# The gain of the first norm: one row spread by a product with ones, and products of the identity ahead of the first tokens

## The chip, the core and the metric

The kernel runs on one NeuronCore of a Trainium2 chip. The metric is the device time of one execution in microseconds. Three runs of the kernel before the change gave 1168.95, 1169.08 and 1169.35 us; the median, 1169.08, is the time before.

## The reference, cut to what matters

One inference step of a hybrid layer, in f32, over 1024 prompt tokens and 8 sample tokens, with 1024 channels:

```
y = xf * lax.rsqrt(jnp.mean(xf * xf, axis=-1, keepdims=True) + EPS) * g      # rms_norm
...
h = rms_norm(x, norm_g)
proj = jnp.einsum('btd,de->bte', h, w_in)
rq, rk, rv, rg, sq, sk, sv, sg, mg_r, mg_s = jnp.split(proj, _split_points(), axis=-1)
rq = rope(rq...); rk = rope(rk...) * (RET_DK ** -0.5)
o_r, ret_state = retention_fn(rq, rk, rv)                                    # branch A, 4 heads
...
y = x + jnp.einsum('btd,de->bte', merged, w_out)
```

The change touches only `norm_g`, the 1024 weights `g` of the first norm: how they come to stand in each of the 128 partitions.

## The kernel before, in words

**Tiles and stages.** The prompt is cut into tiles of 128 tokens, 0 to 7; tile 8 is the 8 sample tokens. `norm_h` (L255) is called once for each. It loads the tile `x` by a DMA on SP's queue (L266), squares it on ScalarE with a sum along the row (L275; two instructions in the trace, the pass and the reading of the sum), makes the root: VectorE the mean (`ms`, L145), GpSimd the power (`rs`, L146). Then VectorE multiplies the tile by the root and by the gain `self.gb` in one pass (L281); for tile 6 alone (`XPOOL`) GpSimd multiplies by the gain (L278) and ScalarE by the root (L279). TensorE transposes the tile in two halves of four products with the identity (L286) into PSUM tiles `tr`, of which there are two. ScalarE copies each half into `hhi`, rounded to the TensorE type fp32r (L138), and VectorE writes what the rounding left out into `hlo` (L139). So each product of activations and weights is made of three: high by high, low by high, high by low.

**The gain.** In tile 0's call, right behind the load of `x`, a DMA reads `norm_g` with a broadcast to 128 partitions into the tile `st` (L267 to L269). All nine tiles use it.

**Weights.** `load_unit` (L150) loads a unit into `wraw` (three buffers), ScalarE writes `whi` (L167), GpSimd `wlo` (L168). The k and v weights of head 0 are four units of 384 KB (128 columns of k, 256 of v, two DMAs each), the q weights one unit of 512 KB.

**Work of TensorE at the start.** For each tile of tokens 24 products of 128x384 (`gemm_tok`, L221 to L223) make k and v; for each block of 344 tokens 24 products of 128x344 (`gemm_T`, L211 to L213) make q, which `ret_q` (L318) turns on VectorE in three passes (L325 to L327) and adds on GpSimd (L328). Both write into PSUM tiles `acc`, of which there are three. Block 0 of q needs the tokens of tiles 0 to 2, block 1 those of tiles 2 to 5. The raw k and v weights of head 0 come a second time as `rraw` (1.5 MB, `load_rows`, L241) for the sample rows, whose products (`quad_rows`, L249) need tile 8. `begin` (L754) sets up the tables; the list `steps` (L787) says in which order the program emits norms, unit loads and tables.

**Order and buffers.** What each engine does in which order is not the order of emission: the framework's scheduler places every instruction when the program is built (`schedule_with_timeline_sim=True`), and the orders are fixed then. Tiles 0 and 1, 2 and 3, 5 and 6, 7 and 8 share a pair buffer `oT` (two of them, `xpair`); tile 4 uses a `qT` buffer. All loads of the start stand in SP's queue, one behind the other.

**Later phases.** Eight groups (four retention heads, four groups of windowed attention) with gates and merge gates, then the branch projections and the output projection.

Of the kernel before, what the change touches and what calls it, by code (L numbers as in the profile page):

```python
# [18 lines left out]
P = 128  # L19
D = 1024  # L20
# [30 lines left out]
NMISC = 8 + 8 + 2 + 2  # L51

RAW = 3
NA1 = 7
XQ = 4
XPOOL = (6,)
# [65 lines left out]
class Body:  # L122
# [27 lines left out]
    def load_unit(self, spec):  # L150
        nc = self.nc
        kind, segs, k0, nk = spec
        width = sum(w for _, _, w in segs)
        raw = self.t(self.wp, [P, D], "wraw", bufs=RAW)
        hi = self.t(self.wp, [P, D], "whi", F32R, bufs=self.wbufs)
# [99 lines left out]
    def norm_h(self, t):  # L255
        nc = self.nc
        p = P if t < NT else NS
        cs = slice(t * P, t * P + p)
# [5 lines left out]
                self.xpair = self.t(self.gp, [P, 2, TOK], "oT", bufs=2)  # L264
            x = self.xpair[:, i % 2, :D]
        nc.sync.dma_start(out=x[:p], in_=self.i["x_prompt"][0, cs, :] if t < NT else self.i["x_sample"][:, 0, :])  # L266
        if t == 0:  # L267
            self.gb = self.t(self.ap, [P, D], "st", bufs=1)
            nc.sync.dma_start(out=self.gb[:], in_=self.i["norm_g"][0:1, :].broadcast_to([P, D]))  # L269
        if t < NT:  # L270
            junk = self.hhi[:, :, cs]
        else:
# [9 lines left out]
        for half in range(2):  # L282
            ps = self.t(self.ptr, [P, 4, P], "tr")
# [433 lines left out]
    def groups(self):  # L717
        nc = self.nc
# [9 lines left out]
        def use(name):  # L728
            if self.apctx is not None:
                self.apctx.__exit__(None, None, None)  # L730
            self.apctx = self.tc.tile_pool(name=name, bufs=1, side="right", reuse_waits="tile") if name else None
            if name:
                self.ap = self.apctx.__enter__()
# [17 lines left out]
        kv = slabs([(OFF_RK, DK), (OFF_RV, DV)])  # L751
        qu = tch(OFF_RQ)

        def begin(us):  # L754
            use("ret")
            self.ropeT = self.t(self.ap, [P, 2, TOK], "ropeT")
            self.ropeK = self.t(self.ap, [P, NT + 1, 128], "ropeK")
            self.maskT = self.t(self.ap, [P, RH, P], "maskT")
            self.kst = self.t(self.ap, [KST, DK], "kst", F32R)
            self.vst = self.t(self.ap, [KST, DV], "vst", F32R)  # L760
            nc.gpsimd.memset(self.kst[:].bitcast(F32), 0.0)
            nc.gpsimd.memset(self.vst[:].bitcast(F32), 0.0)
            self.zq = self.t(self.ap, [P, 2, NS // 2, QD], "zq", bufs=1)
            nc.gpsimd.memset(self.zq[:], 0.0)
# [31 lines left out]
        for gi in range(8):  # L796
            ret = gi < 4
            st = {"v": None}
# [65 lines left out]
        def open_a(us):  # L864
# [3 lines left out]
            self.opA = []  # L868
            for k in range(0, NA1, 2):
                st = self.t(self.gp, [P, 2, TOK], "oT", bufs=2)  # L870
# [162 lines left out]
```

## Time and profile before

| what | value |
|---|---|
| median of the runs | 1169.08 us (1168.95 to 1169.35) |
| profiled execution: its own time, its span | 1167.54 us, 1165.8 us |
| mean granted TensorE clock of it | 0.996 |
| PE busy | 1142.7 us, 98%, 7140 instructions |
| PEld (weight loads) | 1088.8 us, 93% |
| DVE, ACT, POOL | 644.0 us (55%), 437.4 us (38%), 427.5 us (37%) |
| instructions in all | 19287 |
| HBM | 127.8 MB, 110 GB/s over the span |

PE is TensorE, PEld its weight loads, DVE VectorE, ACT ScalarE, POOL GpSimd, SP the engine whose queue issues the loads. A share is that of the whole span; the start of the program, which the change touches, is a few per cent of it and has to be read by itself. The clock is the one that the throttle granted to TensorE, as a share of full speed, 2.4 GHz; the low level is 1.2 GHz.

### The profile page before, as it was taken

The page shows a single profiled execution, that of the slowest core. Times are in us where ns is not written, and L with a number is a line of the kernel's source. Part 1 is how long each engine was busy: PE and PEld are TensorE (multiplying, and loading weights), DVE is VectorE, ACT ScalarE, POOL GpSimd, SP SyncE. Part 2 cuts the span into 40 slices and gives each one's busy share as a digit, 9 for nine tenths or more (in the row PEclk, how much of TensorE's full clock was granted, in tenths as well). Part 3 has the DMA queues.
Part 4 walks back from the last instruction along what each step waited for, and adds up shares of the span by engine and source line. Part 5 has one row for each costly group of instructions (what it writes and reads, how often), then busy time and mean ns, then how long its engine had stood idle before and what let it go on. Part 6 is the DMA issues. An engine that isn't in the chain of part 4 may idle for free.

```text
span 1165.8 us, 19287 instructions
## 1 busy us (share of the span) xinstructions
PE 1142.7 (98%) x7140; PEld 1088.8 (93%) x7140; DVE 644.0 (55%) x1823; ACT 437.4 (38%) x1130; POOL 427.5 (37%) x398
## 2 busy tenths in 40 slices
PE   6899999999999999999999999999999999999998
PEld 5899999999999999999999999999999999999876
DVE  5664645655644487767765776577744411665131
ACT  5444343334344244544463445345544210221010
POOL 4425116316225434634463446235751221221010
PEclk9899999999999999999999999999999999999999
DMA  9434315413123412311141114102437754546431
GB/s 319 124 111 130 115 43 165 154 60 100 47 81 104 141 32 59 91 60 31 34 133 44 33 33 139 38 1 64 151 115 249 230 152 130 179 139 206 158 101 64
DMA packets 135565, 126.99 MB, mean 109 GB/s; under 512 B 17768, under 2 KB 121576, under 8 KB 135440
## 3 DMA queue, kind: packets, MB, share of 16 engines
q1 hardware_dynamic: 128560, 117.32, 32.2%
q10 hardware_dynamic: 6912, 8.46, 2.0%
q8 instruction: 56, 0.92, 0.3%
q14 instruction: 37, 0.30, 0.1%
HBM read 95.37 MB, written 32.44 MB: 110 GB/s over the span
## 4 chain that ended last, share of the span: by engine, by line
PE 90%; DVE 4%; DMA 2%; issue 1%; ACT 1%; POOL 1%; SPq 0%; ACTq 0%; POOLq 0%
PE acc L211 16%; PE acc L212 16%; PE acc L213 15%; PE acc L221 10%; PE acc L223 10%; PE acc L222 10%; PE sc L550 1%; PE sc L551 1%; DMA oT<-in_x_prompt 1%; PE av L583 1%; PE av L582 1%; PE tr L562 1%; DMA oT<-d_o 1%; PE acc L249 1%; PE sc L201 1%
## 5 line engine op out<-in xcount | busy, mean ns | idle before, releaser
L168 POOL TENSOR_TENSOR wlo<-wraw,whi 128x1024 fp32r<-128x1024 f32 (+1 forms) x92 | 205.9, 2245 | 292.3 <-ACT whi L167 291.6
L211 PE MATMUL acc<-hhi,whi 128*128 128x344 f32 x864 | 279.5, 323 | 3.6 <-DVE rng L885 2.5
L212 PE MATMUL acc<-hlo,whi 128*128 128x344 f32 x864 | 277.8, 322 | 0.0
L213 PE MATMUL acc<-hhi,wlo 128*128 128x344 f32 x864 | 276.9, 321 | 0.0
L221 PE MATMUL acc<-whi,hhi 128*128 128x384 f32 x512 | 176.8, 346 | 2.3 <-DVE tg L302 1.2
L222 PE MATMUL acc<-wlo,hhi 128*128 128x384 f32 x512 | 176.1, 344 | 0.0
L223 PE MATMUL acc<-whi,hlo 128*128 128x384 f32 x512 | 175.8, 343 | 0.0
L211 PEld LDWEIGHTS acc<-hhi,whi 128*128 128x128 f32 x864 | 162.4, 188 | 6.1 <-ACT whi L167 2.7
L212 PEld LDWEIGHTS acc<-hlo,whi 128*128 128x128 f32 x864 | 162.4, 188 | 1.7 <-issue 0.4
L213 PEld LDWEIGHTS acc<-hhi,wlo 128*128 128x128 f32 x864 | 162.4, 188 | 1.0
L167 ACT ACTIVATE whi<-wraw 128x1024 fp32r<-128x1024 f32 (+1 forms) x92 | 90.3, 984 | 166.6 <-PE acc L212 110.4
L146 POOL TENSOR_TENSOR rs<-ms,nhalf 128x1 f32<-128x1 f32 (+3 forms) x81 | 68.6, 848 | 229.0 <-DVE ms L145 226.5
L221 PEld LDWEIGHTS acc<-whi,hhi 128*128 128x128 f32 x512 | 97.8, 191 | 5.1 <-issue 1.4
L223 PEld LDWEIGHTS acc<-whi,hlo 128*128 128x128 f32 x512 | 97.9, 191 | 0.9 <-issue 0.4
L222 PEld LDWEIGHTS acc<-wlo,hhi 128*128 128x128 f32 x512 | 98.0, 191 | 0.6 <-issue 0.2
L304 POOL TENSOR_TENSOR oT<-oT,tg 128x344 f32<-128x344 f32 x48 | 48.3, 1007 | 63.1 <-DVE tg L302 52.4
L504 ACT ACTIVATE s<-sc,ng,rs 128x128 f32<-128x128 f32 x128 | 56.9, 455 | 23.1 <-DVE ng L501 22.8
L223 PE MATMUL acc<-whi,mlo 128*128 128x512 f32 x128 | 50.5, 395 | 0.0
L221 PE MATMUL acc<-whi,mhi 128*128 128x512 f32 x128 | 50.4, 394 | 0.0
L222 PE MATMUL acc<-wlo,mhi 128*128 128x512 f32 x128 | 50.3, 393 | 0.0
L1000 DVE TENSOR_TENSOR x<-acc,x 128x512 f32<-128x512 f32 x16 | 11.1, 692 | 71.0 <-PE acc L223 71.0
L302 DVE SCALAR_TENSOR_TENSOR tg<-tg,acc 128x344 f32<-128x344 f32 x48 | 24.5, 510 | 31.8 <-ACT tg L301 31.6
(363 smaller groups left out, 2343.0 us busy)
## 6 DMA issues: line engine op xcount, KB each, us to landing
wraw<-in_w_in SPq DMA_DIRECT2D x36, 512.0 KB
d_t<-tg ACTq DMA_DIRECT2D x48, 172.0 KB
d_o<-oT SPq DMA_DIRECT2D x16, 516.0 KB
tt<-d_t SPq DMA_DIRECT2D x48, 172.0 KB
wraw<-in_w_in SPq DMA_DIRECT2D x32, 256.0 KB
st<-d_o SPq DMA_DIRECT2D x9, 516.0 KB
d_m<-tt SPq DMA_DIRECT2D x24, 172.0 KB
mm<-d_m SPq DMA_DIRECT2D x24, 172.0 KB
```

The costliest lines, as they stand in the source:

```text
L146: nc.gpsimd.tensor_tensor(out=rs[:p, :width], in0=ms[:p, :width], in1=self.nhalf[:p, :width], op=ALU.pow)
L167: nc.scalar.activation(out=hi[:, :f], in_=raw[:, :f], func=AF.Copy)
L168: nc.gpsimd.tensor_tensor(out=lo[:, :f], in0=raw[:, :f], in1=hi[:, :f].bitcast(F32), op=ALU.subtract)
L211: nc.tensor.matmul(ps, whi[:, k, :], hi[:, cs], start=(k == 0), stop=False)
L212: nc.tensor.matmul(ps, whi[:, k, :], lo[:, cs], start=False, stop=False)
L213: nc.tensor.matmul(ps, wlo[:, k, :], hi[:, cs], start=False, stop=(k == KT - 1))
L221: nc.tensor.matmul(ps, hi[:, k, a:b], whi[:, kk, :], start=(k == 0), stop=False)
L222: nc.tensor.matmul(ps, hi[:, k, a:b], wlo[:, kk, :], start=False, stop=False)
L223: nc.tensor.matmul(ps, lo[:, k, a:b], whi[:, kk, :], start=False, stop=(k == KT - 1))
L302: nc.vector.scalar_tensor_tensor(out=tg[:], in0=tg[:], scalar=1.0, in1=ps[:, :BL], op0=ALU.add, op1=ALU.mult)
L304: nc.gpsimd.tensor_tensor(out=sl, in0=sl, in1=tg[:], op=ALU.mult)
L504: nc.scalar.activation(out=s[:p, j, :], in_=src[j], func=AF.Exp, bias=ng[:p, j : j + 1], scale=scale[j], accum_out=l[:p, j : j + 1])
```

## The change

`norm_h` no longer allocates and loads the gain. A new function `spread_gain`, called first in `begin`, does it: one DMA brings `norm_g` as a row of 4 KB into one partition of the tile `zk`, GpSimd writes 128 ones behind it, and two products of the ones (one partition, 128 columns, as weights) with a half of the row (one partition, 512 columns) put the row into every partition of a PSUM tile `sc`, from which VectorE copies it into the two halves of `self.gb`. Beside them `WARM` = 9 products of the identity with itself go into a PSUM tile `av`, whose contents nothing reads. Since `begin` stands ahead of tile 0 in the list of steps, the row's DMA stands ahead of tile 0's.

```diff
--- before.py
+++ after.py
@@ -51,6 +51,7 @@
 NMISC = 8 + 8 + 2 + 2
 
 RAW = 3
+WARM = 9
 NA1 = 7
 XQ = 4
 XPOOL = (6,)
@@ -264,9 +265,6 @@
                 self.xpair = self.t(self.gp, [P, 2, TOK], "oT", bufs=2)
             x = self.xpair[:, i % 2, :D]
         nc.sync.dma_start(out=x[:p], in_=self.i["x_prompt"][0, cs, :] if t < NT else self.i["x_sample"][:, 0, :])
-        if t == 0:
-            self.gb = self.t(self.ap, [P, D], "st", bufs=1)
-            nc.sync.dma_start(out=self.gb[:], in_=self.i["norm_g"][0:1, :].broadcast_to([P, D]))
         if t < NT:
             junk = self.hhi[:, :, cs]
         else:
@@ -751,8 +749,24 @@
         kv = slabs([(OFF_RK, DK), (OFF_RV, DV)])
         qu = tch(OFF_RQ)
 
+        def spread_gain():
+            self.gb = self.t(self.ap, [P, D], "st", bufs=1)
+            row = self.t(self.ap, [1, D + P], "zk", bufs=1)
+            nc.sync.dma_start(out=row[:, :D], in_=self.i["norm_g"][0:1, :])
+            nc.gpsimd.memset(row[:, D:], 1.0)
+            ps = self.t(self.pav, [P, 512], "av")
+            warm = lambda n: [nc.tensor.matmul(ps[:, :P], self.ident[:], self.ident[:], start=True, stop=True) for _ in range(n)]
+            warm(WARM // 3)
+            for half in range(2):
+                cs = slice(half * 512, half * 512 + 512)
+                pg = self.t(self.psc, [P, 512], "sc")
+                nc.tensor.matmul(pg[:], row[:, D:], row[:, cs], start=True, stop=True)
+                nc.vector.tensor_copy(out=self.gb[:, cs], in_=pg[:])
+            warm(WARM - WARM // 3)
+
         def begin(us):
             use("ret")
+            spread_gain()
             self.ropeT = self.t(self.ap, [P, 2, TOK], "ropeT")
             self.ropeK = self.t(self.ap, [P, NT + 1, 128], "ropeK")
             self.maskT = self.t(self.ap, [P, RH, P], "maskT")
```

Line numbers: those of the changed kernel are one higher up to L253, two lower from `norm_h` on, and fourteen higher behind `begin`. The numbers that the framework gives to tiles move as well; each place below says which tiles they are.

The scheduler lays out the whole start anew. Three places show what stands where.

**VectorE, first rows behind the two memsets.** Of the kernel before (`oT_150` holds tiles 0 and 1, `st_152` is the gain, `ms_156`, `ms_185` are the means of tiles 0 and 1):

```order
L145 TENSOR_SCALAR ms_156<-ss_154 128x1
L281 SCALAR_TENSOR_TENSOR oT_150<-oT_150,rs_157,st_152 128x1024
L145 TENSOR_SCALAR ms_185<-ss_183 128x1
L139 TENSOR_TENSOR hlo_122<-tr_161,hhi_121 128x4x128
L281 SCALAR_TENSOR_TENSOR oT_150<-oT_150,rs_186,st_152 128x1024
L139 TENSOR_TENSOR hlo_122<-tr_168,hhi_121 128x4x128
```

Of the changed kernel (`st_141` is the gain, `sc_149` and `sc_152` its halves in PSUM, `ms_174`, `ms_203` and `ms_233` the means of tiles 0 to 2):

```order
L146 TENSOR_SCALAR ms_174<-ss_172 128x1
L146 TENSOR_SCALAR ms_203<-ss_201 128x1
L764 COPY st_141<-sc_149 128x512
L764 COPY st_141<-sc_152 128x512
L279 SCALAR_TENSOR_TENSOR oT_170<-oT_170,rs_175,st_141 128x1024
L279 SCALAR_TENSOR_TENSOR oT_170<-oT_170,rs_204,st_141 128x1024
L146 TENSOR_SCALAR ms_233<-ss_231 128x1
```

The copies of the gain stand behind the mean of tile 1, and the norm of tile 0 behind the copies; before, it stood behind its own mean.

**SP's queue, behind the loads of tiles 0 to 4 and of the first three k and v units.** Of the kernel before (`wraw_241` is the fourth k and v unit, `wraw_273` the q unit, `oT_302` tiles 5 and 6, `oT_349` tiles 7 and 8, `wraw_403` a later gate unit):

```order
L769 DMA ropeT_141<-in_c_ropeT 128x2x344 x2
L161 DMA wraw_241<-in_w_in 128x2x128
L161 DMA wraw_241<-in_w_in 128x2x256
L769 DMA ropeT_141<-in_c_ropeT 128x2x344
L241 DMA rraw_412<-in_w_in 128x8x128
L241 DMA rraw_412<-in_w_in 128x8x256
L161 DMA wraw_273<-in_w_in 128x8x128
L884 DMA rng_111<-in_ret_norm_g 128x8x1
L266 DMA oT_302<-in_x_prompt 128x1024 x2
L161 DMA wraw_403<-in_w_in 128x8x128
L266 DMA oT_349<-in_x_prompt 128x1024
L266 DMA oT_349<-in_x_sample 8x1024
```

Of the changed kernel (`wraw_259` is the fourth k and v unit, `wraw_291` the q unit, `oT_320` tiles 5 and 6, `oT_367` tile 7, `wraw_421` and `wraw_871` later gate units, `wraw_1199` the first unit of the next head):

```order
L162 DMA wraw_259<-in_w_in 128x2x256
L783 DMA ropeT_161<-in_c_ropeT 128x2x344 x3
L162 DMA wraw_291<-in_w_in 128x8x128
L242 DMA rraw_430<-in_w_in 128x8x128
L242 DMA rraw_430<-in_w_in 128x8x256
L898 DMA rng_111<-in_ret_norm_g 128x8x1
L162 DMA wraw_421<-in_w_in 128x8x128
L267 DMA oT_320<-in_x_prompt 128x1024 x2
L162 DMA wraw_871<-in_w_in 128x8x128
L162 DMA wraw_1199<-in_w_in 128x2x128
L162 DMA wraw_1199<-in_w_in 128x2x256
L267 DMA oT_367<-in_x_prompt 128x1024
```

The q unit has moved ahead of `rraw`; the gate unit has moved ahead of tiles 5 and 6; and one gate unit of 512 KB and a unit of 384 KB now stand ahead of tile 7, where one gate unit stood.

**VectorE and TensorE at tiles 5 to 8.** VectorE of the kernel before (`oT_302` with `rs_307` is tile 5, `tr_311` and `tr_318` its transposes, `oT_349` with `rs_354` tile 7 and with `rs_377` tile 8, `acc_495` block 0 of q):

```order
L281 SCALAR_TENSOR_TENSOR oT_302<-oT_302,rs_307,st_152 128x1024
L145 TENSOR_SCALAR ms_329<-ss_327 128x1
L145 TENSOR_SCALAR ms_353<-ss_351 128x1
L145 TENSOR_SCALAR ms_376<-ss_374 8x1
L139 TENSOR_TENSOR hlo_122<-tr_311,hhi_121 128x4x128
L281 SCALAR_TENSOR_TENSOR oT_349<-oT_349,rs_354,st_152 128x1024
L139 TENSOR_TENSOR hlo_122<-tr_318,hhi_121 128x4x128
L281 SCALAR_TENSOR_TENSOR oT_349<-oT_349,rs_377,st_152 8x1024
L325 TENSOR_TENSOR qT_410<-acc_495,ropeT_141 128x344
L326 TENSOR_TENSOR ropeu_520<-acc_495,ropeT_141 64x344
L327 TENSOR_TENSOR ropeu_520<-acc_495,ropeT_141 64x344
```

VectorE of the changed kernel (`oT_320` with `rs_325` is tile 5, `tr_329` and `tr_336` its transposes, `tr_306` and `tr_313` those of tile 4, `oT_367` with `rs_372` tile 7 and with `rs_395` tile 8, `acc_513` block 0 of q):

```order
L324 TENSOR_TENSOR ropeu_538<-acc_513,ropeT_161 64x344
L325 TENSOR_TENSOR ropeu_538<-acc_513,ropeT_161 64x344
L279 SCALAR_TENSOR_TENSOR oT_320<-oT_320,rs_325,st_141 128x1024
L146 TENSOR_SCALAR ms_347<-ss_345 128x1
L140 TENSOR_TENSOR hlo_122<-tr_306,hhi_121 128x4x128
L146 TENSOR_SCALAR ms_371<-ss_369 128x1
L279 SCALAR_TENSOR_TENSOR oT_367<-oT_367,rs_372,st_141 128x1024
L146 TENSOR_SCALAR ms_394<-ss_392 8x1
L140 TENSOR_TENSOR hlo_122<-tr_313,hhi_121 128x4x128
L279 SCALAR_TENSOR_TENSOR oT_367<-oT_367,rs_395,st_141 8x1024
L140 TENSOR_TENSOR hlo_122<-tr_329,hhi_121 128x4x128
L140 TENSOR_TENSOR hlo_122<-tr_336,hhi_121 128x4x128
```

TensorE of the changed kernel (`acc_604` is block 1 of q, `tr_353` the first half of tile 6):

```order
L284 MATMUL tr_329<-ident_63,oT_320 128x128 x4
L284 MATMUL tr_336<-ident_63,oT_320 128x128 x4
L212 MATMUL acc_604<-hhi_121,whi_292 128x344
L284 MATMUL tr_353<-ident_63,oT_320 128x128 x4
L213 MATMUL acc_604<-hlo_122,whi_292 128x344
L214 MATMUL acc_604<-hhi_121,wlo_293 128x344
L212 MATMUL acc_604<-hhi_121,whi_292 128x344
```

Block 0's rope now stands ahead of tile 5's norm, both norms of the second pair ahead of tile 5's low halves, and a half of tile 6's transposes between block 1's first and second product.

## Rows read from the trace of the kernel before

**Rows 1.** Stretch, length, busy PE, PEld, DVE, ACT, POOL, clock, DMA share, GB/s.
```profile
8.00:17.00 9.00, 7.91 (x29) 7.20 (x30) 4.64 (x7) 7.29 (x12) 7.43 (x5) 1.00 1.05 391
26.00:30.00 4.00, 1.52 (x11) 1.25 (x10) 3.93 (x17) 2.77 (x7) 0.03 (x1) 1.00 1.14 305
30.00:35.00 5.00, 5.00 (x20) 5.00 (x21) 2.26 (x2) 3.75 (x6) 5.00 (x3) 0.66 1.11 328
50.00:60.00 10.00, 10.00 (x59) 8.51 (x59) 5.33 (x21) 3.43 (x10) 0.00 (x0) 0.83 0.18 48
60.00:80.00 20.00, 20.00 (x135) 19.32 (x134) 12.44 (x47) 8.55 (x27) 6.10 (x8) 1.00 0.35 109
```

**Rows 2.** Timeline (start, duration, engine, operation, [idle before, releaser]): the first `rraw` product.
```profile
50.03 0.83 PE L249 MATMUL acc<-rraw,hx 128*8 128x384 f32 x8
```

**Rows 3.** Timeline: products of 128x384 in and behind slow stretches.
```profile
16.21 0.52 PE L222 MATMUL acc<-wlo,hhi 128*128 128x384 f32 x1
...
34.35 0.34 PE L223 MATMUL acc<-whi,hlo 128*128 128x384 f32 x1
```

**Rows 4.** Timeline, 28 to 36 us: block 0 of q, tiles 5 to 7.
```profile
28.84 1.05 ACT L167 ACTIVATE whi<-wraw 128x1024 fp32r<-128x1024 f32 x1
...
29.94 0.42 PE L211 MATMUL acc<-hhi,whi 128*128 128x344 f32 x1 [2.48 <-DVE rng L885]
...
29.97 2.39 POOL L168 TENSOR_TENSOR wlo<-wraw,whi 128x1024 fp32r<-128x1024 f32 x1 [5.02 <-ACT whi L167]
...
32.33 0.54 POOL L146 TENSOR_TENSOR rs<-ms,nhalf 128x1 f32<-128x1 f32 x1
...
32.84 2.39 POOL L278 TENSOR_TENSOR oT<-oT,st 128x1024 f32<-128x1024 f32 x1
32.90 3.42 DVE L281 SCALAR_TENSOR_TENSOR oT<-oT,rs,st 128x1024 f32<-128x1024 f32 x1 [1.60 <-POOL rs L146]
...
33.09 1.06 ACT L167 ACTIVATE whi<-wraw 128x1024 fp32r<-128x1024 f32 x1 [0.62 <-DMA wraw<-in_w_in]
...
34.56 1.06 ACT L275 ACTIVATE hhi<-oT 128x1024 fp32r<-128x1024 f32 x1 [0.41 <-DMA oT<-in_x_prompt]
```

**Rows 5.** Timeline, 0 to 10 us: the first loads and norms.
```profile
0.80 0.40 SPq L266 DMA_DIRECT2D oT<-in_x_prompt  x1
...
1.26 0.42 SPq L269 DMA_DIRECT2D st<-in_norm_g  x1
...
1.69 0.29 POOL masks.py:199 TENSOR_SCALAR_AFFINE_SELECT ident<-ident 128x128 f32<-128x128 f32 x1
...
4.56 1.06 ACT L275 ACTIVATE hhi<-oT 128x1024 fp32r<-128x1024 f32 x1 [2.48 <-DMA oT<-in_x_prompt]
...
6.80 1.28 DVE L281 SCALAR_TENSOR_TENSOR oT<-oT,rs,st 128x1024 f32<-128x1024 f32 x1 [0.90 <-DMA st<-in_norm_g]
...
9.37 1.06 ACT L275 ACTIVATE hhi<-oT 128x1024 fp32r<-128x1024 f32 x1 [0.41 <-DMA oT<-in_x_prompt]
```

**Rows 6.** Chain of waits (start, duration, what): two f32 products of 128x128.
```profile
60.73 0.22 PE av L391 x2
```

**Rows 7.** Timeline, 38 to 46 us: tiles 5 and 7, block 1 of q.
```profile
38.78 0.69 DVE L139 TENSOR_TENSOR hlo<-tr,hhi 128x512 fp32r<-128x512 f32 x1 [1.85 <-ACT hhi L138]
...
39.98 1.28 DVE L281 SCALAR_TENSOR_TENSOR oT<-oT,rs,st 128x1024 f32<-128x1024 f32 x1 [0.51 <-POOL rs L146]
...
40.59 0.60 PE L286 MATMUL tr<-ident,oT 128*128 128x128 f32 x4
...
40.94 0.40 PE L212 MATMUL acc<-hlo,whi 128*128 128x344 f32 x1
...
44.60 0.92 POOL L328 TENSOR_TENSOR qT<-qT,ropeu 128x344 f32<-128x344 f32 x1 [4.15 <-DVE ropeu L327]
...
44.94 0.31 PE L213 MATMUL acc<-hhi,wlo 128*128 128x344 f32 x1
...
45.76 0.51 DVE L325 TENSOR_TENSOR qT<-acc,ropeT 128x344 f32<-128x344 f32 x1
```

## The prediction

> **What bounds the kernel now.** I read the stretches first (busy time by window), then the start instruction by instruction. In the stretches [rows 1] the reader is to see that TensorE is busy 20.00 of 20.00 us from 60 us on, so nothing later can give time back, and that it is not full before: 7.91 of 9.00 us at 8 to 17, 1.52 of 4.00 at 26 to 30. The order of every engine is the same in both programs from about 100 us on, so the change is worth what it shifts the moment from which TensorE stays full. I take that moment at the first product on `rraw`, at 50.03 us [rows 2], with the same work done before it in both programs (tiles 0, 1, 2 of k and v, blocks 0 and 1 of q, all transposes).
>
> Three stretches run at 1.2 GHz. Single matmuls show it: 128x384 takes 0.52 us at 16.21 and 0.34 at 34.35 [rows 3]; the clock column of the first stretch reads 1.00 all the same, so there the rows of single matmuls decide. At 30 to 35 us the mean granted clock is 0.66, which is 3.4 us at half speed, and 0.83 at 50 to 60 is 3.4 us again [rows 1], which costs 1.7 us where TensorE is the bound. Before the spell at 31 us TensorE had stood idle for 2.48 us [rows 4].
>
> **The gain of the norm.** Before, its 512 KB stand second in SP's queue: issued at 1.26, and VectorE starts tile 0's norm at 6.80, the end of a wait for it [rows 5]. Tile 0 itself had landed at 4.56, so the broadcast held the queue for 2.24 us. Removed, everything behind it comes up to 2.24 us earlier, less 0.46 us because the row of 4 KB is now issued ahead of tile 0 (the step from 0.80 to 1.26 [rows 5]): 1.8 us.
>
> In its place stand nine products of the identity, two of ones with the row, and two copies. No row shows a product of 128x512 f32 on one partition. The nearest is the f32 product of 128x128, two instructions in 0.22 us at the high clock [rows 6]: 0.44 at the low one. Nine are 4.0 us; they begin when the identity is written (1.69 + 0.29 [rows 5]) and end at 6.0. The spread ones have four times the columns, 1.76 us each at the low clock and 0.88 at the high; by partitions used it could be less, not more. I take 1.76, since 8 to 17 us ran low after TensorE had begun: 7.8 and 9.5. The copies pass 512 columns out of PSUM as the 0.69 us pass does [rows 7]. On VectorE they stand behind tile 1's mean: tile 1 landed at 9.37 [rows 5], now 7.6, and its square takes 1.2, so the first copy starts at 8.9 and the second ends at 10.2. Then tile 0's norm, 1.28, would be done at 11.5 against 8.08. GpSimd's split of a weight unit lies beside it; a VectorE pass with two inputs in SBUF beside GpSimd's product of 2.39 us took 3.42 us [rows 4], so 12.8 is the upper end. Tile 0 comes **3.4 to 4.7 us later**, though its weights are there earlier.
>
> What hides that: q's weight unit (512 KB) now goes ahead of the 1.5 MB of `rraw`. Before, block 0 of q waited for it (weights at 28.84, TensorE idle 2.48 us to 29.94 [rows 4]) and block 0 with tile 2 ended at about 40.4, since the transposes behind block 1's first product start at 40.59 [rows 7]. Without that wait it is 37.9, and with the full 4.7 us on top 42.6. That is still no cost, if what follows it starts later than 42.6; it does.
>
> **Tile 5 and block 1 of q.** Block 1 needs tile 5. Before, tile 5's low half is made (0.69 us at 38.78) ahead of the norms of tiles 7 (39.98) and 8, and the block's second matmul runs at 40.94 [rows 7]. Now it stands behind both norms on VectorE, and TensorE has tile 6's transposes between the first and second matmul of the block, which need the buffer that this low half frees. The chain, from rows:
>
> Tile 5's norm ends at 36.3 (32.90 + 3.42 [rows 4]) as before: the unit that now stands just ahead of it in SP's queue has the place that q's had, with the same bytes ahead, so its split on GpSimd (29.97 + 2.39) and the product of tile 6 (to 35.2) stay where they are. Bounds: 34.5 if all of the 1.8 us reaches it, 37.2 if block 0's rope on VectorE, which now precedes it, is late. I take 36.3, by the bytes. GpSimd then has block 0's rope sum, 0.92 [rows 7], and two powers of 0.54 [rows 4]: 38.3. Tile 7 has 384 KB more ahead of it than before; 512 KB took 1.5 us there (33.09 to 34.56 [rows 4]), so it lands 1.1 us later, at 35.7, and its square is done at 36.9, inside 38.3. Tile 7's norm: 39.6. Tile 4's last low half 0.69, and a short mean: 40.5. Tile 8's norm 1.28: 41.8. Tile 5's low half 0.69: 42.5. Four transposes, 0.60 [rows 7]: the second matmul at **43.1 against 40.94, 2.2 us later**.
>
> From there to 50.03 the same matmuls and transposes follow. Two things differ. Before, block 1 ended at 45.25 and its rope began at 45.76, VectorE being busy; now it is free: 0.5 us back. And TensorE stands idle from the end of tile 2 (37.9 to 42.6) to 43.1, in the middle of that range about as long as the 2.48 us that preceded the spell at 31 us. I take the longer half, and so a low spell in block 1: 1.7 us. The spell after 50 us stays, since the idle time ahead of it is that of tiles 7 and 8 in both.
>
> **Sum**: 2.2 - 0.5 + 1.7 = 3.4 us later. The profiled execution took 1167.54 us, so 1170.9; the median of the runs shown stands 1.5 us above it, so **1172.5**. A measurement of this kernel can tell some 0.2%, 2.3 us, from no change. With the ends for tile 5 (1.8 earlier, 0.9 later) the sum goes from 1.6 to 4.3.
>
> **The rivals.**
> *The clock holds.* Block 1 finds the high clock, or the spell after 50 us does not return: 3.4 - 1.7 = 1.7 us, 1170.8, no difference that can be told. For it: TensorE's wait before block 1 may be as short as 0.5 us. Against: at 26 to 30 us a wait of 2.48 us was enough [rows 1, 4].
> *The front carries through* (faster). Transfers 2.24 us earlier move tile 5's norm as much, and block 0 ends early enough that its rope sum on GpSimd, 0.92, no longer stands ahead of tile 7's power. Then the second matmul runs at 40.0, and with the clock high in block 1 and after 50 us the sum is 2.2 - 2.24 - 0.92 - 0.5 - 1.7 = -3.2 us, 1165.9. It decides whether tile 7's norm begins before 35.5 us. For it: SP's queue is what tiles wait for at the start [rows 5]. Against: tile 5 has the same bytes ahead as before.
> The Trainium skill's page "TensorE: Matmul & The Clock Gate", in its Part 1, says that the array starts throttled and that activity releases it, so that products issued ahead should let the first tiles run at 2.4 GHz. By that rule the 7.91 busy us at 8 to 17 [rows 1] would take half, 3.95 us less, and if all of that reached the end the time would be 1165.1. The trace agrees that this stretch runs low, but not that its speed bounds anything: block 0 waited for weights at its end.
> *The front is late as well* (slower still). Tile 0 at 12.8 or later leaves tiles 0 and 1 at the low clock again, block 0 ends after 36, its rope holds tile 5's norm and the chain behind it by some 2 to 3 us more: about 6 us, 1175.1.
>
> **How the numbers follow.** Forecast 0.48, the clock holds 0.23, the front carries 0.17, the front is late 0.12. Slower is the forecast and the late front, 0.60; same 0.23; faster 0.17. The likeliest case gives 1172.5, its own range 1170.7 to 1173.4. The range of 1167.0 to 1176.0 leaves out the faster rival, and goes a little past the late front's 1175.1, whose lateness is only bounded loosely.
>
> **What would show it.** Right: tile 0's norm from about 10.3 us, tile 5's low half at about 41.8, block 1's second matmul near 43 at 0.29 us spacing, the first `rraw` product at 53 to 54. Wrong: tile 7's norm before 37, or block 1 at 0.16 us spacing from its start; and if TensorE had gaps past 100 us that it did not have before, the whole argument by a shift would fall.

## The result and the profile after

The changed kernel takes 1176.59 us (median of 4 runs, 1175.48 to 1177.58) against 1169.21 before: a ratio of 1.0060, 95% interval 1.0042 to 1.0077, so 7.4 us slower. The prediction had 1172.5 and a range that ended at 1176.0.

The profiled execution took 1177.58 us, span 1175.8. Stretches, answering to [rows 1] and in the same columns:

```profile
8.00:17.00 9.00, 2.87 (x10) 2.06 (x10) 6.93 (x7) 5.99 (x10) 6.59 (x5) 0.53 1.05 386
26.00:30.00 4.00, 4.00 (x28) 3.93 (x27) 2.98 (x11) 1.28 (x3) 2.32 (x1) 1.00 1.18 264
30.00:35.00 5.00, 5.00 (x35) 4.95 (x35) 2.66 (x10) 4.54 (x8) 2.75 (x2) 1.00 1.09 342
40.00:45.00 5.00, 1.89 (x9) 1.28 (x8) 4.30 (x6) 3.08 (x7) 1.57 (x4) 0.77 0.01 2
45.00:50.00 5.00, 5.00 (x22) 4.94 (x22) 0.99 (x2) 0.65 (x2) 0.00 (x0) 0.55 0.40 105
50.00:55.00 5.00, 2.91 (x23) 2.57 (x21) 3.51 (x6) 2.02 (x5) 0.92 (x1) 1.00 0.01 2
55.00:60.00 5.00, 4.23 (x20) 2.76 (x21) 2.23 (x13) 1.33 (x7) 0.45 (x1) 0.66 0.01 3
60.00:80.00 20.00, 20.00 (x128) 18.27 (x127) 14.91 (x46) 8.25 (x26) 4.08 (x5) 1.00 0.27 79
```

The stall that stood at 26 to 30 us is gone, and so is the low clock at 30 to 35. In their place TensorE works 1.89 us of the five from 40 on, and the five behind them run at a granted clock of 0.55. From 60 us on it is full again, as before.

The timeline of the start, answering to [rows 5] and [rows 3]:

```profile
1.92 3.80 PE L758 MATMUL av<-ident 128*128 128x128 f32 x18 [1.92 <-POOL ident masks.py:199]
...
4.91 1.06 ACT L273 ACTIVATE hhi<-oT 128x1024 fp32r<-128x1024 f32 x1 [2.82 <-DMA oT<-in_x_prompt]
...
5.65 1.98 PE L763 MATMUL sc<-zk 1*128 1x512 f32 x4
...
8.77 1.06 ACT L273 ACTIVATE hhi<-oT 128x1024 fp32r<-128x1024 f32 x1 [0.53 <-DMA oT<-in_x_prompt]
...
10.03 1.28 DVE L764 COPY st<-sc 128x512 f32<-128x512 f32 x2
...
11.41 5.11 DVE L279 SCALAR_TENSOR_TENSOR oT<-oT,rs,st 128x1024 f32<-128x1024 f32 x2
...
16.17 0.52 PE L223 MATMUL acc<-wlo,hhi 128*128 128x384 f32 x1
```

The nine products end at 5.72 us, the spread at 7.63. The gain is ready on TensorE then, but VectorE's copies stand behind tile 1's mean and start at 10.03. The first transposes run at 13.82, after 6.20 us without work, and the products behind them at the low clock.

The chain of waits through tiles 7, 8 and 5, answering to [rows 7] (start, duration, what):

```profile
32.37 0.45 PE tr L284 x4
32.83 5.24 DMA oT<-in_x_prompt
...
40.97 1.05 ACT oT L277
42.25 0.55 POOL rs L147
42.83 1.27 DVE oT L279
44.10 0.61 DVE hlo L140
44.76 1.12 PE tr L284 x4
45.87 0.29 PE acc L213
```

And the instructions themselves, from the timeline; the row at 56.42 answers to [rows 2]:

```profile
32.26 2.39 POOL L169 TENSOR_TENSOR wlo<-wraw,whi 128x1024 fp32r<-128x1024 f32 x1 [3.93 <-ACT whi L168]
...
32.57 1.06 ACT L273 ACTIVATE hhi<-oT 128x1024 fp32r<-128x1024 f32 x1 [0.39 <-DMA oT<-in_x_prompt]
...
34.60 0.55 POOL L147 TENSOR_TENSOR rs<-ms,nhalf 128x1 f32<-128x1 f32 x1
...
35.03 0.52 DVE L323 TENSOR_TENSOR qT<-acc,ropeT 128x344 f32<-128x344 f32 x1
...
36.63 2.17 DVE L279 SCALAR_TENSOR_TENSOR oT<-oT,rs,st 128x1024 f32<-128x1024 f32 x1
...
37.68 1.91 POOL L326 TENSOR_TENSOR qT<-qT,ropeu 128x344 f32<-128x344 f32 x1
...
38.10 1.06 ACT L273 ACTIVATE hhi<-oT 128x1024 fp32r<-128x1024 f32 x1 [2.37 <-DMA oT<-in_x_prompt]
...
39.55 1.06 POOL L147 TENSOR_TENSOR rs<-ms,nhalf 128x1 f32<-128x1 f32 x2
...
40.65 1.47 DVE L279 SCALAR_TENSOR_TENSOR oT<-oT,rs,st 128x1024 f32<-128x1024 f32 x1 [1.11 <-POOL rs L147]
...
45.52 0.64 PE L213 MATMUL acc<-hlo,whi 128*128 128x344 f32 x1
...
51.77 0.32 PE L214 MATMUL acc<-hhi,wlo 128*128 128x344 f32 x1
...
56.42 1.47 PE L250 MATMUL acc<-rraw,hx 128*8 128x384 f32 x8
...
61.33 0.81 PE L250 MATMUL acc<-rraw,hx 128*8 128x384 f32 x2
...
62.85 0.82 PE L250 MATMUL acc<-rraw,hx 128*8 128x384 f32 x6
```

And tile 5's square in the kernel before, beside the row at 32.57:

```profile
29.96 1.06 ACT L275 ACTIVATE hhi<-oT 128x1024 fp32r<-128x1024 f32 x1
```

The reader is to see two things. The first is that tile 5 is late already: the split that stands ahead of its power on GpSimd begins at 32.26 (29.97 before, [rows 4]), and ScalarE waits for tile 5's load until 32.57, where before it squared the tile at 29.96 without such a wait. The second is the order of the chain: tile 7's norm (40.65, after a wait for its power on GpSimd), tile 8's (42.83), tile 5's low half (44.10), then four transposes at the low clock (1.12 us against 0.60), then block 1's second product at 45.52 against 40.94. The first `rraw` product is at 56.42 against 50.03.

How much of it stays is read from one instruction far behind the start: VectorE's second rope pass of the last q block of head 1, at 207.00 us before and 214.46 now.

```profile
214.46 0.52 DVE L324 TENSOR_TENSOR ropeu<-acc,ropeT 64x344 f32<-64x344 f32 x1
```

This **shift** of 7.46 us stays within 0.05 us from 174 to 380 us. It agrees with the medians (7.4 us). The profiled executions themselves differ by 10.0. What goes beyond the shift lies behind 380 us: in this execution TensorE waits 2.1 us for the operands of the branch projection (the two rows below, of the waits behind 100 us) where the profile of before has none.

```profile
PE acc L212 <- ACT opA6h L925: 1.2, 1, 1.2
...
PE acc L213 <- DVE opA6l L926: 0.9, 1, 0.9
```

So the table of the experiments gives both: the ratio over the runs, and the shift of this one instruction in the one trace that each kernel has. One run each of e7, e9, e12 and e16 took far longer than the others (1253.95 to 6419.66 us) and is left out of the medians and ratios; the trace of e16 is of such a run, so it has no shift.

### The profile page after: what moved, and what is told of

Same layout as the page of the kernel before. It is cut to its first block, busy times and chain, and to the rows that moved or that the text cites. A ratio compares the mean times of both kernels' runs of the same rounds, so it can differ in the third digit from the quotient of the medians.

```text
span 1175.8 us, 19338 instructions
## 1 busy us (share of the span) xinstructions
PE 1150.1 (98%) x7162; PEld 1093.6 (93%) x7162; DVE 649.6 (55%) x1825; ACT 437.5 (37%) x1130; POOL 427.3 (36%) x399
## 4 chain that ended last, share of the span: by engine, by line
PE 91%; DMA 3%; DVE 3%; ACT 1%; issue 1%; POOL 1%; SPq 0%; ACTq 0%; POOLq 0%
PE acc L212 16%; PE acc L213 16%; PE acc L214 16%; PE acc L222 10%; PE acc L223 10%; PE acc L224 10%; PE sc L548 1%; PE sc L549 1%; DMA oT<-d_o 1%; DMA wraw<-in_w_in 1%; PE av L580 1%; PE av L581 1%; PE tr L560 1%; PE acc L250 1%; PE sc L202 1%
## 5 line engine op out<-in xcount | busy, mean ns | idle before, releaser
L983 DVE SCALAR_TENSOR_TENSOR tt<-tt,acc 128x344 f32<-128x344 f32 x24 | 12.0, 513 | 55.2 <-DMA tt<-d_t 50.3
```

What stands on the lines that cost most here:

```text
L983: nc.vector.scalar_tensor_tensor(out=tt[:], in0=tt[:], scalar=1.0, in1=ps[:, :BL], op0=ALU.add, op1=ALU.mult)
```

## The experiments

Two questions: is it what the change adds that costs, or the order into which the scheduler laid the start? And which place of it? To hold an order, a kernel is given edges between neighbours of the wanted order on each engine; they fix the order of issue and add no wait (`info` has the class `NoSync`).

```python
for e, runs in ORDER.items():
    at = [k for r in runs.split() for a, b in [(r + "-" + r).split("-")[:2]] for k in range(int(a), int(b) + 1)]
    for a, b in zip(at, at[1:]):
        self.tc.add_manual_dep(ins[e][b], ins[e][a].name, info, reason="pin")
```

`ins[e]` are the instructions of an engine as the program emits them, and `ORDER` names them by that count, for some 530 instructions of TensorE, 185 of VectorE, 120 of ScalarE, 52 of GpSimd and 44 loads: all of the stretch in which the two orders differ. The edges themselves cost nothing that shows: e15, the kernel before held in its own order with nine products more, starts `rraw` at 50.10 against 50.03. The cuts of `ORDER` below name the engine ahead of the numbers where it isn't in the text.

| run | what | median us | ratio to before, 95% | shift us | first `rraw` us |
|---|---|---|---|---|---|
| e1 | before, order of the change | 1177.20 | 1.0068 (1.0055 to 1.0081) | +8.31 | 57.22 |
| e2 | change, order of before | 1170.30 | 1.0006 (0.9996 to 1.0016) | +1.95 | 52.02 |
| e3 | change, copies first | 1175.30 | 1.0047 (1.0035 to 1.0059) | +7.05 | 55.96 |
| e4 | change, `WARM` = 0 | 1175.45 | 1.0051 (1.0039 to 1.0063) | +5.67 | 54.88 |
| e5 | before, loads of the change | 1173.37 | 1.0032 (1.0022 to 1.0042) | +4.03 | 53.27 |
| e6 | before, computing order of the change | 1178.76 | 1.0082 (1.0069 to 1.0096) | +10.42 | 59.33 |
| e7 | change, tile 3 in one piece | 1175.89 | 1.0057 (1.0042 to 1.0072) | +7.32 | 56.21 |
| e8 | row, no products, order of before | 1170.03 | 1.0006 (0.9996 to 1.0017) | +0.98 | 50.12 |
| e9 | change, tile 5 first | 1172.94 | 1.0038 (1.0023 to 1.0052) | +3.97 | 52.88 |
| e10 | change, its gaps filled | 1175.15 | 1.0054 (1.0041 to 1.0068) | +5.08 | 54.00 |
| e11 | before, both gaps filled | 1167.00 | 0.9979 (0.9970 to 0.9987) | -1.36 | 50.19 |
| e12 | e9, loads and tile 3 as well | 1172.72 | 1.0028 (1.0017 to 1.0039) | +4.27 | 53.19 |
| e13 | e8, both gaps filled | 1166.50 | 0.9980 (0.9970 to 0.9991) | -1.67 | 49.85 |
| e14 | e12, copies first as well | 1172.88 | 1.0031 (1.0019 to 1.0042) | +2.70 | 51.62 |
| e15 | before, the late gap filled | 1166.25 | 0.9974 (0.9965 to 0.9983) | -1.45 | 50.10 |
| e16 | change again | 1175.25 | 1.0047 (1.0034 to 1.0060) | | |

### Order, or what is added: e1, e2

e1 is the kernel before with the order of the change (its broadcast stays second in the queue); e2 the change with the order of before, the copies right behind tile 0's mean.

```diff
                 self.phase23()
+        self.pin()
```

> The kernel before, the gain still loaded by the broadcast, with the first instructions of all five engines held in the order of the changed kernel. Order theory (the order of tiles 5 to 8 and of the loads is what costs): 3 to 7 us slower than before, the first product on rraw at 53 to 56 us. Late-gain theory (the two copies behind tile 1's mean hold tile 0's norm, and that runs through to the end): no copies here, tile 0's norm done near 8 us, so within 1.5 us of before, rraw at 49 to 51.5 us.

> The changed kernel, the row spread by products and the nine products of the identity kept, held in the order of the kernel before on all five engines; the copies stand right behind tile 0's mean. Order theory: within 1.5 us of before, rraw at 49 to 51.5 us. Clock theory (nine products long before the first tokens leave a gap behind them, and the array is low at tiles 0 and 1): tile 0's norm done near 10.3 us, the products of tile 0 low until 19 us or later, 2 to 4 us slower than before whatever the order.

Measured: 1.0068 and 1.0006. The kernel before loses in the new order at least what the change lost, with no instruction of the change in it (a little more than the order theory expected, `rraw` at 57.22); and the change in the old order loses nothing that its runs can tell, though its one trace stands 1.95 us later and starts `rraw` at 52.02, 0.5 us later than the order theory expected. **The loss is the order.** What e1 was expected to show by the late-gain theory was wrong in one point: it has no copies, and its tile 0 is late all the same. VectorE of e1, timeline:

```profile
10.51 0.15 DVE L173 TENSOR_SCALAR ms<-ss 128x1 f32<-128x1 f32 x1 [4.75 <-ACT hhi L303]
10.64 1.28 DVE L309 SCALAR_TENSOR_TENSOR oT<-oT,rs,st 128x1024 f32<-128x1024 f32 x1
```

In the new order tile 1's mean stands ahead of tile 0's norm, so tile 0 waits for tile 1 to land, gain or no gain.

### The front: e3, e4

e3 moves the two copies (numbers 2 and 3 of VectorE) ahead of tile 1's mean (8); e4 takes the nine products away and lets the scheduler lay the start out.

```diff
-  1 4 8 2-3 5 9
+  1 4 2-3 8 5 9
...
-WARM = 9
+WARM = 0
```

> The changed kernel in its own order on all engines, with one difference: VectorE makes the two copies of the gain right behind tile 0's mean and not behind tile 1's. Late-gain theory: tile 0's norm done at 10.3 instead of 13.8 us, and most of the loss gone: within 2 us of before. Order theory: the front is early but tiles 5 to 8 are where they were in the changed kernel, 3 us or more slower than before.

> The changed kernel with WARM = 0: no products of the identity, the scheduler lays the start out anew (q's unit still ahead of rraw, both norms of tiles 7 and 8 around tile 5's low half, as in the changed kernel). Clock theory: with no products ahead the gain is spread 2 us earlier and tile 0's norm is done at 8 to 9 us; the clock is low at tile 0 as before; within 1.5 us of before. Order theory: tile 5 and block 1 stay late, 2 to 4 us slower than before.

Measured: 1.0047 and 1.0051, hardly below the change itself (1.0060, and 1.0047 in its second series, e16). In e3 tile 0's norm ends at 11.26 us and not near 13.8, and the shift is 0.4 us less: an early front alone buys next to nothing. In e4 tile 0 is done at 8.27, nearly as before, and the shift is still 5.67; at the medians the loss is 5.6 us, more than either theory expected. The nine products are not the cause either, though e4 has an order of its own and not the change's.

### Loads or computing order: e5, e6, e7

e5 and e6 hold one half of the kernel before in the order of the change (e5 the loads, e6 the four computing engines). The order of one computing engine alone was not exchanged: each order waits for results that the other engines give in the same one, so that they could wait in a circle. e7 moves tile 3's second half (numbers 39 to 42 of TensorE) behind its first, so that the pair buffer for tile 7 is free earlier.

```diff
-  37-38 131-143 160-161 39-42 144-145
+  37-42 131-143 160-161 144-145
```

> The kernel before with SP's queue alone in the order of the changed kernel (q's unit ahead of rraw, one gate unit ahead of tiles 5 and 6, a gate unit and a unit of the next head ahead of tile 7); the four computing engines in the order of before. Load theory (tile 7 comes late because more bytes stand ahead of it): tile 7 lands at 37 to 38 us instead of 34.6, the first product on rraw 2 to 3 us late, 2 to 4 us slower than before. Compute-order theory (VectorE, TensorE, ScalarE and GpSimd take tiles 5 to 8 in a worse order): within 1.5 us of before.

> The counterpart: the kernel before with TensorE, VectorE, ScalarE and GpSimd in the order of the changed kernel and SP's queue as before. Compute-order theory: 5 to 7 us slower than before, tile 5's low halves still behind the norms of tiles 7 and 8. Load theory: tile 7 lands near 35 us, its norm and tile 8's come 2 to 3 us earlier than in the changed kernel, and the time is at most 4 us above before.

> The changed kernel in its own order with one move: on TensorE the second half of tile 3's transposes stands right behind the first half, ahead of block 0 of q, so that the pair buffer that tile 7's load waits for comes free near 30 us and not at 32.8. Buffer theory (tile 7 is late because its load waits for that buffer): tile 7 lands 2 us earlier, near 36, and the time falls by 1.5 to 3 us below the changed kernel's. Byte theory (what stands ahead in the queue decides): it lands less than 1 us earlier, and the time stays within 1 us of the changed kernel's.

Measured: 1.0032, 1.0082 and 1.0057. The loads alone do cost: tile 7 lands at 38.54 instead of 34.56, and `rraw` starts 3.24 us late. The computing order costs more, and dearest with loads that were laid out for the other one: e6 is 9.8 us slower at the medians, more than either theory expected, and its tile 7 lands at 40.44. The two don't add up (4.03 and 10.42 against 8.31 together): each half of an order seems to be made for its other half. In e7 tile 7's load is issued at 30.26 instead of 32.83 and lands at 36.96 instead of 38.10, and the shift moves by 0.14 us. The landing moved by 1.14 us, more than the byte theory expected and less than the buffer theory; the time moved as the byte theory had it. When tile 7 lands is not what decides here: its norm waits for its power, which stands on GpSimd behind block 0's rope sum (37.68 to 39.59 in the change), and in e7 it starts only 0.36 us earlier, at 40.29.

### The place: e9, e12, e14

e9 takes tile 5 ahead in the change's own order: on VectorE the low halves of tile 4's second half (23) and of tile 5 (26, 27) go ahead of tile 7's mean and norm (31, 32) and tile 8's (35, 36); on ScalarE the high halves (19, 21, 22) go behind tile 7's square (27); on TensorE tile 6's transposes (59 to 62) behind seven more products of block 1.

```diff
-  VectorE 28 22 31-32 35 23 36 26-27 29-30
+  VectorE 28 22-23 26-27 31-32 35-36 29-30
...
-  ScalarE 18 27 30 51 19 24 21-22 25-26
+  ScalarE 18 27 19 21-22 30 51 24-26
...
-  TensorE 58 184 59-62 185-193
+  TensorE 58 184-191 59-62 192-193
```

> The changed kernel in its own order, with tile 5 taken ahead on three engines: VectorE makes the low halves of tile 4's second half and of tile 5 before the norms of tiles 7 and 8, ScalarE their high halves right behind tile 7's square, TensorE puts tile 6's first transposes behind six products of block 1. If the low halves behind those norms are the step that costs: block 1's second product at 42 to 43 us instead of 45.5, the time 2.5 to 4 us below the changed kernel's. If tile 7's and 8's lateness sets the end whatever stands at tile 5: block 1 earlier, but the first rraw product not before 55 us, the time within 1 us of the changed kernel's.

Measured: 1.0038; the shift falls from 7.46 to 3.97. In the ratio the gain is 2.2 thousandths against the change's first series and 0.9 against its second, and the intervals overlap; so the place rests on the traces. Timeline of e9:

```profile
40.81 0.69 DVE L168 TENSOR_TENSOR hlo<-tr,hhi 128x512 fp32r<-128x512 f32 x1 [0.35 <-ACT hhi L167]
...
41.56 0.43 PE L241 MATMUL acc<-hlo,whi 128*128 128x344 f32 x1 [0.23 <-DVE hlo L168]
...
43.32 1.47 DVE L307 SCALAR_TENSOR_TENSOR oT<-oT,rs,st 128x1024 f32<-128x1024 f32 x1 [0.73 <-POOL rs L175]
45.50 1.27 DVE L307 SCALAR_TENSOR_TENSOR oT<-oT,rs,st 8x1024 f32<-8x1024 f32 x1 [0.65 <-POOL rs L175]
```

Block 1's second product is at 41.56, 0.6 us from where it was before the change, and the block runs at the high clock. But the norms of tiles 7 and 8 now come 2.7 us later than in the change, and the `rraw` products need tile 8: they start at 52.88.

e12 adds the loads of tiles 7 and 8 ahead of the gate unit and the next head's unit, and e7's move; e14 adds e3's copies to that.

```diff
-  SP 18 20 29 33-34 21-22 37-38
+  SP 18 20-22 29 33-34 37-38
```

> The changed kernel in its own order with the repair of tile 5 and, besides, the loads of tiles 7 and 8 ahead of the gate unit and the unit of the next head, and tile 3's transposes in one piece so that the buffer is free. If loads and order at tiles 5 to 8 together are the loss: tile 7 lands near 36 us or earlier, the first rraw product at 51 to 53 us, the time 4 to 6 us below the changed kernel's and 1 to 3 above before. If the late front (tile 0's norm done at 13.8 us) is the larger part: not more than 3 us below the changed kernel's.

> The changed kernel in its own order with every repair: the copies right behind tile 0's mean, tile 5's low halves ahead of the norms of tiles 7 and 8, tiles 7 and 8 loaded ahead of the gate unit and the next head's unit, tile 3's transposes in one piece. If the late front is the rest of the loss: the first rraw product at 50.5 to 52 us, the time 0.5 to 2 us above before. If something else in the new order holds the end (the split of the second four rraw products, norms 7 and 8 now behind tile 5): rraw not before 52.5 us, 2.5 us or more above before.

Measured: 1.0028 and 1.0031. In e12 tile 7 lands at or before 35.74 and the shift doesn't fall (4.27 against 3.97): behind tile 5 the loads no longer decide. In e14 the early front, worth 0.4 us alone, is worth 1.6 (4.27 to 2.70): in the traces it pays once tile 5 doesn't hide it. The runs don't show it: the ratio doesn't fall from e12 to e14, and both kernels stand 3.3 to 3.6 us above before, more than their expectations gave the repair. 2.70 us of shift are left. Of these 1.59 are there at the first `rraw` product (51.62), with tile 8's norm at 44.23 against 41.78; the rest comes behind it, where the second four `rraw` products are still split. No run took these two apart, so how the last 2.70 divide stays open.

### The clock: e8, e10, e11, e13, e15

e8 has the row and neither products nor the new order. The others put products of the identity where TensorE waits: e10 in the change's gaps ahead of tile 5's second transposes and tile 6's first (10 and 4), e11 and e13 in the gap ahead of block 0 (11) and around the transposes of tiles 7 and 8 (9), e15 only these nine.

```diff
+            for _ in range(GAP):
+                nc.tensor.matmul(ps[:, :P], self.ident[:], self.ident[:], start=True, stop=True)
```

> The row spread by products, WARM = 0, all engines held in the order of the kernel before, the two copies ahead of tile 0's mean. If the products of the identity are what the row's way costs beside the order: tile 0's norm done near 8.3 us (before 8.1, with them and in the old order 11.1), the first rraw product at 49.5 to 50.5 us, the time from 1 us below before to 0.5 above. If the way through the row itself is dearer, the norm is at 9 us or later and the time 1 to 2 us above.

> The changed kernel in its own order with 14 more products of the identity on TensorE, ten in the gap before tile 5's second transposes (40.2 to 42.8 us) and four in the gap before tile 6's (43.6 to 44.8). Clock theory: the array stays high, block 1 runs at 0.16 us spacing from its start, which gives back about 1.8 us of block 1 and 0.5 of the transposes; the time is 1.5 to 2.5 us below the changed kernel's. If block 1's speed is hidden by a later wait (tile 8's rows): block 1 is faster, rraw starts within 0.5 us of 56.4, the time within 0.7 us.

> The kernel before in its own order with 20 products of the identity in its gaps: eleven while block 0 waits for its weights (27.5 to 29.9 us), nine around the transposes of tiles 7 and 8 (46.5 to 49.8 us). Clock theory: the low stretches at 31 to 34.4 and 50.8 to 54.9 us vanish; the first is hidden behind tile 5, the second was on the path that sets the end: 1.5 to 2 us faster than before. If the fill delays the transposes more than the clock gives back: within 0.7 us of before or slower.

> The row spread by products, no products ahead of it, all engines in the order of the kernel before, the copies ahead of tile 0's mean, and the 20 products of the identity in the gaps (eleven before block 0, nine around the transposes of tiles 7 and 8). If the fill alone gives the gain: as fast as the kernel before with the fill, 1.5 to 3 us below before. If the row adds what it brings the queue: another 0.3 to 0.6 us.

> The kernel before in its own order with nine products of the identity around the transposes of tiles 7 and 8 alone, and none ahead of block 0. If only the low stretch behind the first rraw product is on the path that sets the end: as fast as with all 20 products, 1.5 to 2.5 us below before, while 31 to 34 us run low as before. If the first stretch counts as well: less than 1 us below before.

Measured: 1.0006, 1.0054, 0.9979, 0.9980 and 0.9974. e11, e13 and e15 are **faster than both kernels**, than the kernel before by 2.3 to 3.0 us in the ratio; their traces show 1.4 to 1.7 of that as a shift. The transposes and `rraw` products of e15, timeline:

```profile
46.46 1.50 PE L799 MATMUL av<-ident 128*128 128x128 f32 x12
...
49.10 0.94 PE L799 MATMUL av<-ident 128*128 128x128 f32 x6
...
50.10 0.83 PE L278 MATMUL acc<-rraw,hx 128*8 128x384 f32 x8
```

Stretches: 50 to 55 us of the kernel before, then two of e15.

```profile
50.00:55.00 5.00, 5.00 (x24) 4.33 (x24) 1.26 (x7) 0.66 (x2) 0.00 (x0) 0.66 0.01 3
...
30.00:35.00 5.00, 5.00 (x29) 5.00 (x30) 2.19 (x2) 3.44 (x6) 4.99 (x3) 1.00 1.12 327
50.00:55.00 5.00, 5.00 (x39) 3.47 (x37) 2.14 (x11) 1.53 (x5) 0.00 (x0) 1.00 0.01 3
```

`rraw` starts where it did before (50.10 against 50.03), but the stretch from 50 to 55 us has a granted clock of 1.00 and holds 39 products, where before it had 0.66 and 24. Filling the gap ahead of block 0 as well (e11) adds nothing that the runs can tell. What the low clock at 31 us costs, these runs don't show: in e15 that stretch ran at 1.00 too, against the expectation, with nothing put into the gap of 2.48 us ahead of it. The row adds at most 0.3 us in the shift (e13), which the runs can't tell from nothing; nor does e8 alone differ from before. Its one trace has `rraw` at 50.12, as before, and the 0.98 us of its shift come behind, where the clock from 50 to 55 us is 0.50. In the old order the nine products at the start (e2 has them, e8 not; e8 also makes the copies ahead of tile 0's mean) stand for 1.90 us at the first `rraw` product in the traces, and for nothing in the ratios (1.0006 both).

In e10 block 1 runs at 0.16 us spacing from its second product on and `rraw` starts 2.4 us earlier than in the change. But the low clock then comes behind it, as its stretches show:

```profile
40.00:45.00 5.00, 4.47 (x39) 4.09 (x37) 4.35 (x6) 3.01 (x7) 2.47 (x3) 1.00 0.01 4
45.00:50.00 5.00, 5.00 (x37) 4.83 (x35) 1.73 (x4) 1.79 (x3) 0.00 (x0) 1.00 0.35 105
50.00:55.00 5.00, 2.14 (x20) 1.13 (x19) 4.34 (x16) 2.12 (x8) 1.36 (x2) 1.00 0.01 2
55.00:60.00 5.00, 5.00 (x19) 4.06 (x18) 0.42 (x1) 0.08 (x1) 0.00 (x0) 0.66 0.00 0
```

Most of its 2.14 busy us from 50 to 55 are tile 8's transposes and the first `rraw` products, with waits of 2.04 and 0.70 us between that nothing was put into, and 0.66 follows. In the trace the clock in block 1 was a real term (a shift of 5.08 against 7.46). The runs don't show it: the ratio is 0.6 of a thousandth below the change's first series and 0.7 above its second, far from the 1.5 to 2.5 us that the clock theory expected.

e16, the change once more beside e13 to e15:

> The changed kernel itself once more, beside the others on the same chip: 6.5 to 8 us slower than before, as in the first comparison.

Measured: 1.0047, 6.0 us at the medians, a little under the expected range.

## Why the prediction was wrong

The direction and the place held: tile 5's low halves behind the norms of tiles 7 and 8, then a low clock in block 1. The size did not, because the chain through that place began later than the prediction let it. Term by term, against the trace of the change:

- **The front** was to bring tile 0 3.4 to 4.7 us later; it came 5.7 later (transposes at 13.82 against 8.14). The spread products were half as dear as taken, 0.99 us each and not 1.76. By its own rows the upper end was too low: 10.2 and a pass of 3.42 make 13.6 for the end of tile 0's norm, not 12.8. And tile 1 landed at 8.77 and not at 7.6: without the broadcast it came 0.6 us earlier, where 1.8 were reckoned. The norms of tiles 0 and 1 shared VectorE's time with GpSimd's splits, 5.11 us for the two.
- **Its cover** held: block 0 and tile 2 ended at 39.3, inside 37.9 to 42.6, although the front came later than its upper end, and e3 shows that an earlier front would have bought 0.4 us.
- **The step that failed** is that tile 5's norm "ends at 36.3 (32.90 + 3.42 [rows 4]) as before", since the unit ahead of it has "the same bytes ahead, so its split on GpSimd (29.97 + 2.39) and the product of tile 6 (to 35.2) stay where they are". The norm ended at 38.80. The same bytes were not the same time: the split began at 32.26, tile 5 landed at 32.57, its power was there at 35.15, and tile 6's product ended at 37.73. The broadcast that is gone from the queue had held back little by then (e8, the row in the old order: q's split at 29.72 against 29.97), so it did not make up for the q unit that now stands ahead. With an early front (e3) the split begins at 31.09; how the 2.29 us divide between loads and front is not shown beyond that. Block 0's rope also stood ahead of the norm on VectorE, from 35.03 to 36.60, but it is the smaller part: e2, with the rope behind as before, has the split at 31.95 and the norm's end at 38.30 (the rows below). From there GpSimd carried the lateness on: after tile 6's product the rope sum took 1.91 us and not 0.92, and the powers ended at 40.61, where the sum had 38.3. Everything that follows kept the chain's own lengths: tile 7's norm at 42.1 (39.6 predicted), tile 8's at 44.1 (41.8), tile 5's low half at 44.7 (42.5), the second product at 45.52 (43.1). The 2.2 us of the sum measured 4.58.

```profile
31.95 2.40 POOL L197 TENSOR_TENSOR wlo<-wraw,whi 128x1024 fp32r<-128x1024 f32 x1 [5.02 <-ACT whi L196]
...
34.90 3.40 DVE L307 SCALAR_TENSOR_TENSOR oT<-oT,rs,st 128x1024 f32<-128x1024 f32 x1 [1.79 <-POOL rs L175]
```

- **Tile 7's landing** was put at 35.7 by 384 KB more ahead of it; it was 38.10. Its load could not be issued before 32.83, when tile 3's transposes released the pair buffer, a wait that the prediction did not have. e7, which takes 2.57 us of that wait away, moves the shift by 0.14 us.
- **The rope that finds VectorE free**: 0.5 us back predicted; from block 1's end to `rraw` it is 4.33 us against 4.78, so 0.45.
- **The clock in block 1**: 1.7 us predicted; from the second product to the block's end it took 6.57 us against 4.31, so 2.26, of which half a tile of transposes that now stands inside the block is some 0.5. By e10 the stretch does recover its clock when the gap is filled. The reason given, that a wait of 2.48 us "was enough", is no rule: e8 and e15 have the same wait ahead of block 0 and no low stretch behind it.
- **What was not in the sum**: that the work behind the first `rraw` product differs too. The second four `rraw` products stand together before and as one and three now, 0.81 and 0.82 us where 0.83 covered all four; and the first four ran at the low clock (1.47 against 0.83). Together with a shorter low stretch behind, this is what is left of the shift: 7.46 less 6.39, 1.07 us.

4.58 - 0.45 + 2.26 + 1.07 = 7.46 us.

Of the rivals, "the front is late as well" (6 us, 0.12) came nearest in its number, and it named the late norm of tile 5; but block 0 ended at 34.99 and not after 36, and tile 0's lateness did not carry it: with tile 0 early in e3 the loss stayed. So its 1175.1, 1.5 us from the measured median, is near by luck. The faster rival needed tile 7's norm before 35.5 us; it began at 40.65. Of the signs of being wrong one did come, waits of TensorE past 100 us that were not there before (2.1 us in the two rows of the waits): the shift describes the trace up to 380 us and not to its end.

On the Trainium skill's page "TensorE: Matmul & The Clock Gate", Part 1: by its rule that activity releases the throttle and idleness brings it back, products issued ahead should help. The trace agrees with the second half. Nine products that end at 5.72, with the spread at 7.63 and 6.20 us of nothing behind them, left tile 0's products at 0.52 us; nine products right around the wait that precedes the work (e15) left the work at 1.00.

## What to carry to other kernels

Where a scheduler lays out the program, a small change at the start is a change of the whole order: hold the old order and run the new instructions in it, and hold the new order and run the old ones, before anything is said about the instructions themselves. In the chain, look for work that the next block needs (tile 5's low half) and that stands behind work that is needed only later (the norms of tiles 7 and 8): a norm that waits for its load or its power holds everything behind it in its engine's fixed order. A load with the same bytes ahead of it need not land at the same time. And products that keep the clock up paid here in the last gap before the work that sets the end, not at the start of the program.

## What the runs showed of the hardware that was not expected

- Removing a load of 512 KB from the second place in the queue brought the next loads forward by 0.6 to 0.7 us (tile 1 at 8.77 against 9.37, the first weight unit at 7.40 against 8.11), not by the 2.24 us between the landing of the tile ahead of it and the norm that waited for it; tile 0 itself landed at 4.91 against 4.56. Far behind it, at the split of the q unit in the old order, 0.25 us were left (e8, 29.72 against 29.97).
- The same idle time does not always bring the low clock: TensorE stands idle for 2.48 us ahead of block 0 in the kernel before, e2 and e5, and products at the low clock follow (from 31.15, 32.54 and 31.28 us on); in e8 and e15 it stands idle for 2.48 us as well, and the clock from 30 to 35 us is 1.00.
- Four products of 8 sample columns with 384, on four column positions, take 0.83 us together; one of them alone takes 0.81 ([rows 2], and the row at 61.33 of the change). The Trainium skill's page "TensorE: Matmul & The Clock Gate", Part 3, says that products at different tile positions run at the same time in one array; the two rows agree, and show what it costs to part them.
- Nine f32 products of the identity, 2.44 us of work in e15's two rows (1.50 and 0.94) whose result nothing reads, make a kernel of 1169 us faster by 2.6 thousandths (0.9974, 0.9965 to 0.9983).
